# A three-block opening, a refetched half group and a shift added by TensorE in a hybrid encoder block

## The chip, the cores and the metric

The kernel runs on one core of a Trainium2 chip. The metric is the time of one execution on the device in microseconds (us). Engines are called by their names: TensorE (PE) multiplies matrices, with its weight loads shown apart as PEld; VectorE (DVE) and ScalarE (ACT) work element by element; GpSimd (POOL) does so too; SyncE (SP) issues transfers from memory. The profile also shows the clock that was granted to TensorE, as a share of the full one.

## What is computed

One layer of an encoder on 256 tokens of 2048 channels, in float32. The reference, cut to its skeleton:

```python
proj = h @ w_in[l]
q, k, v, r, af, ab, hy_u, gate_logits = jnp.split(proj, split_idx, axis=-1)
y_gla = _gla_branch(q, k, v, r, af, ab, ...)      # gated linear attention, both directions
y_hy = _hyena_branch(hy_u, ...)                   # two long convolutions by FFT, gated
g = jax.nn.sigmoid(gate_logits...)
merged = g[:, :, 0, :] * (y_gla @ w_gla_o[l]) + g[:, :, 1, :] * (y_hy @ w_hy_o[l])
mix = merged @ w_out[l]
h = _layernorm(DEEPNORM_ALPHA * h + mix, ln1_g[l], ln1_b[l])
ff = jnp.square(jax.nn.relu(h @ w_ff1[l])) @ w_ff2[l]
h = _layernorm(DEEPNORM_ALPHA * h + ff, ln2_g[l], ln2_b[l])
```

Nearly all of the arithmetic is in products with weight matrices. The two layer norms stand where all channels of a token must be known before anything can go on.

## The kernel before

The tokens form two tiles of 128. All weights lie in memory as blocks of 128 x 2048 numbers (1 MB each), in the order in which they are used. `fetch` (line 89) brings the next block into one of three `raw` buffers by a transfer on SP's queue and splits each half of it in two (`split_hi_lo`, line 80): ScalarE rounds the half to a shorter format (`whi`), and VectorE subtracts that from the original (`wlo`). There are three buffers for split halves. A product then takes a high and a low part, so that float32 accuracy comes from fast products: hi x hi, hi x lo and lo x hi.

There are two ways to use a block. `channel_pair` (line 133) makes channels by tokens: a pair of products for each of the 16 k tiles, one 512 wide (lines 143 and 373: both parts of the activations at once) and one 256 wide (lines 144 and 374). `token_group` with `token_products` (line 151) makes tokens by channels: 512 channels from four blocks, three 512-wide products for each k tile and token tile. `column_products` (line 778) does the same with 256 channels at a time. `fetch`ing runs one block ahead of the products, and side work (filters, attention, convolutions) is hung onto the stream of blocks by `later` and `pump`: each block counts as one tick. The order of the instructions on each engine is then set by a scheduler that simulates a timeline, so source order is not instruction order, but on each engine the order is fixed.

The stages that matter here, in order:

- Opening (lines 209 to 221 and 367 to 378). Three warm-up products; then block 0 and x in halves on SP, the block's first half, then two quarters of x, and so on. x becomes `xT`, split in two parts. The products of block 0 (`pa`) follow k tile by k tile; blocks 1 and 2 are the first two of q. `filt_consts` (line 237) loads nine small constants by ScalarE's queue.
- Filters and attention: `filt_layer`, `filt_time` and `filt_freq` make the long filters beside the q, k and r blocks; the attention runs beside the v blocks.
- Inverse transform (`hy_inv`, line 650): 16 times, 12 products of 256 columns, six for each token tile.
- w_out and the first norm (lines 803 to 834): groups 0 to 2 of four blocks each, for both token tiles; group 3 keeps three of its blocks resident in split form (`resident`, line 743), so that tile 0 can be finished ahead of tile 1, 256 channels at a time. `add_mix` adds the residual and takes statistics, `norm_scale` (line 760) makes scale and shift, `norm_chunk` (line 771) applies them: one ScalarE step, then a multiplication by the row ln1_g and an addition of ln1_b on VectorE, for one chunk of 512 channels on POOL. `turn` transposes a chunk on TensorE and splits it into `hT`.
- ff1 and ff2 in quarters. The first block of ff1 takes tile 0 first and tile 1 then (`by_tile`).
- End (lines 874 to 886): the last group of ff2, with four resident blocks, tile 0 and then tile 1; the second norm by the same `norm_chunk`, and six stores for each tile.

Of the kernel before, what the change touches and what calls it, by code (L numbers as in the profile page):

```python
# [16 lines left out]
P = 128  # L17
# [23 lines left out]
def block_kernel(  # L41
# [42 lines left out]
    nblk = wblk.shape[0]  # L84
# [4 lines left out]
    def fetch(between=lambda n, h: None):  # L89
        n = fetched[0]  # L90
        if n >= stop_at[0]:
            return
        fetched[0] = n + 1
        raw = wp.tile([P, D], F32, tag="raw", bufs=3, name=f"raw{n}")
        if n > 1:
            nc.sync.dma_start(raw, wblk[n])
        parts = []
        for h in range(2):
            if n <= 1:
                hs = slice(h * D // 2, (h + 1) * D // 2)  # L100
                nc.sync.dma_start(raw[:, hs], wblk[n][:, hs])
                between(n, h)
            hi = wp.tile([P, D // 2], F32R, tag="whi", bufs=3, name=f"whi{n}_{h}")
            lo = wp.tile([P, D // 2], F32R, tag="wlo", bufs=3, name=f"wlo{n}_{h}")
            split_hi_lo(hi, lo, raw[:, h * 1024:(h + 1) * 1024])
            parts.append((hi, lo))
        queue.append(parts)

# [24 lines left out]
    def channel_pair(act, name, dst=None, scale=1.0, by_tile=False):  # L133
        if dst is None:
            dst = base.tile([P, 2, L], F32, tag="sum", name=f"{name}_s")
        for c in range(2):
            ps = psum_main(f"{name}_{c}").rearrange("p (a b) -> p a b", a=2)
            parts = next_block()
            for ts in ((slice(0, P), slice(P, L)) if by_tile and c == 0 else (slice(0, L),)):
                for kt in range(KT):  # L140
                    hi, lo = parts[kt // 8]
                    js = slice(kt % 8 * P, (kt % 8 + 1) * P)
                    MM(ps[:, :, ts], hi[:, js], act[:, kt, :, ts], start=(kt == 0), stop=False)  # L143
                    MM(ps[:, 0, ts], lo[:, js], act[:, kt, 0, ts], start=False, stop=(kt == KT - 1))  # L144
            low = base.tile([P, L], F32, tag="low", name=f"{name}_l{c}")
            nc.scalar.activation(low, ps[:, 1], AF.Copy, scale=scale)
            nc.vector.scalar_tensor_tensor(dst[:, c], ps[:, 0], scale, low, op0=ALU.mult, op1=ALU.add)
            pump()
        return dst
# [58 lines left out]

    with tc.tile_pool(name="xp", bufs=1) as xp:
        def load_x(n, h):  # L210
            for g in (2 * h, 2 * h + 1):
                xr = xp.tile([P, 4, L], F32, tag=f"xr{g}", name=f"xr{g}")
                nc.sync.dma_start(xr, xt[:, 4 * g:4 * g + 4, :])
                split_hi_lo(xT[:, 4 * g:4 * g + 4, 0], xT[:, 4 * g:4 * g + 4, 1], xr)
# [6 lines left out]
        fetch(load_x)  # L221
# [15 lines left out]
    def filt_consts():  # L237
        raw = fp.tile([P, 4, P], F32, tag="w4", name="dftraw")
        nc.scalar.dma_start(raw, dft_in)
        split_hi_lo(dfth, dftl, raw)  # L240
        mw = fp.tile([P, 3, P], F32, tag="mlpw", name="mlpw")
        nc.scalar.dma_start(mw, mlp_w)
        mc = fp.tile([P, 4], F32, tag="mlpc", name="mlpc")
        nc.scalar.dma_start(mc, mlp_c)
        et = fp.tile([P, L], F32, tag="emb", name="emb_sb")
        nc.scalar.dma_start(et, emb)
        nc.scalar.dma_start(ba_sb, ba)
        nc.scalar.dma_start(conv_sb, convp)
        nc.scalar.dma_start(mask_sb, mask_in)
        nc.scalar.dma_start(sgn_sb, sgn_in)  # L250
        nc.scalar.dma_start(ident, ident_in)
        fst["mw"], fst["mc"], fst["g"] = mw, mc, et
# [113 lines left out]

    pa = psum_main("pa").rearrange("p (a b) -> p a b", a=2)
    fetch()
    parts = next_block()
    for kt in range(KT):  # L370
        hi, lo = parts[kt // 8]
        js = slice(kt % 8 * P, (kt % 8 + 1) * P)
        MM(pa, hi[:, js], xT[:, kt], start=(kt == 0), stop=False)
        MM(pa[:, 0], lo[:, js], xT[:, kt, 0], start=False, stop=(kt == KT - 1))
# [7 lines left out]
    k_sb = qp.tile([P, 8, L], F32, tag="k", name="k_sb")  # L382
    for dst, nm, sc in ((q_sb, "q", 1.0 / 16.0), (k_sb, "k", 1.0)):
        for c2 in range(4):
            channel_pair(xT, f"{nm}{c2}", dst[:, 2 * c2:2 * c2 + 2, :], sc)
# [357 lines left out]
    def resident(slots):  # L743
        parts = []
        for hi, lo in slots:
# [3 lines left out]
            nc.sync.dma_start(raw, wblk[n])  # L749
# [18 lines left out]

    CHUNKS = ((0, 256), (256, 256), (1536, 512), (512, 512), (1024, 256), (1280, 256))

    def norm_chunk(z, rows, tb, at, n, rs, nb):
        zc = z[:, tb, at:at + n]
        eng = nc.gpsimd if at == 1536 else nc.vector
        nc.scalar.activation(zc, zc, AF.Identity, scale=rs, bias=nb)
        eng.tensor_tensor(zc, zc, rows[:, 0, at:at + n], op=ALU.mult)
        eng.tensor_tensor(zc, zc, rows[:, 1, at:at + n], op=ALU.add)
# [26 lines left out]
    for g in range(3):  # L803
        pss = token_group(mT, f"wo{g}")
        for tb in range(NT):
            add_mix(pss[tb], tb, g * 512, 512)
    x0 = tuple(ep.tile([P, D], F32R, tag=t, name=t) for t in ("xh", "xl"))
    parts = resident([x0] + halves(ep, "f", "wr1"))
    pss = [[psum_main(f"wo3_{tb}{ch}") for ch in range(2)] for tb in range(NT)]
    column_products(pss, mT, [queue.popleft()], range(NT), 0)  # L810
    stop_at[0] = nblk
    hT = act_tile(ep, "hT", "hT")
    for tb in range(NT):
        column_products(pss, mT, parts, [tb], 1)
        if tb == 1:
            fetch()
# [12 lines left out]

        for at, n in CHUNKS:  # L830
            norm_chunk(z1, rows1, tb, at, n, rs, nb)
            if at < 1536:
                turn(at, n)
        turn(1536, 512)
# [4 lines left out]
    def ff1(qi):  # L839
        f = act_tile(ep, "f", f"f{qi}") if qi % 2 == 0 else act_tile(base, "xT", f"f{qi}")  # L840
        for c2 in range(8):
            r = channel_pair(hT, f"f{qi}_{c2}", by_tile=(qi == 0 and c2 == 0))
# [7 lines left out]
    def add_ff(ps, tb, at, n, qi):  # L850
# [26 lines left out]
    pss = [[psum_main(f"w2_33_{tb}{ch}") for ch in range(2)] for tb in range(NT)]  # L877
    for tb in range(NT):
        column_products(pss, fts[3], parts, [tb], 0)
        with tc.high_priority():  # L880
            for ch in range(2):
                add_ff(pss[tb][ch][:, 0:256], tb, 1536 + ch * 256, 256, 3)
            rs, nb = norm_scale(st2, tb, "2")
        for at, n in CHUNKS:
            norm_chunk(z1, rows2, tb, at, n, rs, nb)
            nc.sync.dma_start(out[tb * P:(tb + 1) * P, at:at + n], z1[:, tb, at:at + n])
# [127 lines left out]
```

## Time and profile before

| | us |
|---|---|
| median of 3 runs | 1893.24 (1892.57 to 1893.65) |
| the profiled execution | 1891.83 |
| its span, first to last instruction | 1890.0 |
| TensorE busy | 1860.4 |
| VectorE busy | 1313.6 |
| ScalarE busy | 949.5 |
| POOL busy | 38.3 |
| moved from and to memory | 375.09 MB, 198 GB/s on average |

The mean granted clock is 0.994. In rows of the timeline the columns are: start, duration, engine, line, operation, output <- input, shape, count, and in brackets the idle time of the engine just before and what ended it. In rows of windows: the stretch, its length, the busy time of PE, PEld, DVE, ACT and POOL with the number of instructions, the granted clock, the share of the DMA engines and GB/s. A row of a group has busy time and mean duration in ns. Products overlap in the records; what one costs is seen from start to start.

### The profile page before, as it was taken

How to read it: one execution, taken by the hardware profiler on the slowest of the kernel's cores; microseconds unless marked ns; L12 is line 12 of the kernel's file. 1: busy time of each engine (PE TensorE's matmuls, PEld its weight loads, DVE VectorE, ACT ScalarE, POOL GpSimd, SP SyncE). 2: the span in 40 equal slices, each digit the busy share in tenths (PEclk: the TensorE clock that was granted, in tenths of full speed). 3: DMA queues.
4: the chain of work that ended last, by engine and by line, in shares of the span. 5: the costliest groups of instructions: out<-in, count | busy, mean ns of one | idle time of the engine just before them, and what ended most of it. 6: DMA issues, size and time to landing. Idle time of an engine off the chain costs nothing.

```text
span 1890.0 us, 25333 instructions
## 1 busy us (share of the span) xinstructions
PE 1860.4 (98%) x10060; PEld 1599.7 (85%) x10060; DVE 1313.6 (70%) x1702; ACT 949.5 (50%) x1286; POOL 38.3 (2%) x60
## 2 busy tenths in 40 slices
PE   8999999999999999999999998999999999999996
PEld 7887888888888888888888888888888888888886
DVE  6787968875789888888556567666555555555556
ACT  5555556674555555555544444444434443444343
POOL 0000000000000000000000001000000000000001
PEclk9999999999999999999999999999999999999998
DMA  7667764445555555565655764555555555545552
GB/s 289 231 225 251 265 228 161 140 142 204 195 195 199 199 194 189 197 223 191 212 197 183 285 216 153 188 193 186 196 186 198 180 199 187 192 180 199 191 189 110
DMA packets 60583, 375.09 MB, mean 198 GB/s; under 512 B 7216, under 2 KB 10928, under 8 KB 20912
## 3 DMA queue, kind: packets, MB, share of 16 engines
q1 hardware_dynamic: 46512, 324.03, 47.4%
q0 software_dynamic: 5888, 29.36, 4.2%
q10 hardware_dynamic: 8064, 20.07, 3.0%
q8 instruction: 79, 1.29, 0.3%
q14 instruction: 40, 0.33, 0.0%
HBM read 356.66 MB, written 16.78 MB: 198 GB/s over the span
## 4 chain that ended last, share of the span: by engine, by line
PE 93%; DVE 4%; ACT 1%; DMA 1%; issue 1%; ACTq 0%; DVEq 0%; SPq 0%
PE f L143 13%; PE f L144 6%; PE g L143 6%; PE w L163 6%; PE w L164 6%; PE w L162 6%; PE go L143 3%; PE ux L143 3%; PE uz L143 3%; PE uv L143 3%; PE g L144 3%; PE ho L143 3%; PE ho L144 2%; PE uv L144 2%; PE ux L144 2%; PE go L144 2%
## 5 line engine op out<-in xcount | busy, mean ns | idle before, releaser
L82 DVE TENSOR_TENSOR wlo<-raw,whi 128x1024 fp32r<-128x1024 f32 x596 | 728.3, 1223 | 488.2 <-ACT whi L81 487.3
L81 ACT CAST whi<-raw 128x1024 fp32r<-128x1024 f32 x596 | 627.0, 1053 | 772.6 <-PE w L164 186.8
L143 PE MATMUL f<-hT,whi 128*128 128x512 f32 (+1 forms) x1040 | 361.7, 394 | 0.0
L144 PE MATMUL f<-hT,wlo 128*128 128x256 f32 (+1 forms) x1040 | 290.0, 279 | 0.0
L143 PEld LDWEIGHTS f<-hT,whi 128*128 128x128 f32 x1040 | 195.6, 188 | 44.3
L144 PEld LDWEIGHTS f<-hT,wlo 128*128 128x128 f32 x1040 | 197.1, 190 | 0.1
L163 PE MATMUL w<-wlo,f 128*128 128x512 f32 x480 | 186.8, 389 | 0.0
L164 PE MATMUL w<-whi,f 128*128 128x512 f32 x480 | 186.8, 389 | 0.0
L143 PE MATMUL g<-xT,whi 128*128 128x512 f32 x512 | 178.6, 393 | 0.0
L162 PE MATMUL w<-whi,f 128*128 128x512 f32 x480 | 168.0, 389 | 0.0
L144 PE MATMUL g<-xT,wlo 128*128 128x256 f32 x512 | 143.5, 281 | 0.0
L143 PEld LDWEIGHTS g<-xT,whi 128*128 128x128 f32 x512 | 95.7, 187 | 21.1
L162 PEld LDWEIGHTS w<-whi,f 128*128 128x128 f32 x480 | 90.0, 188 | 18.8
L164 PEld LDWEIGHTS w<-whi,f 128*128 128x128 f32 x480 | 90.1, 188 | 18.7
L163 PEld LDWEIGHTS w<-wlo,f 128*128 128x128 f32 x480 | 90.1, 188 | 18.5
L144 PEld LDWEIGHTS g<-xT,wlo 128*128 128x128 f32 x512 | 96.7, 189 | 0.5 <-DVE wlo L82 0.2
L143 PE MATMUL uz<-xT,whi 128*128 128x512 f32 x256 | 91.9, 398 | 0.0
L143 PE MATMUL ux<-xT,whi 128*128 128x512 f32 x256 | 91.7, 398 | 0.0
L143 PE MATMUL go<-yg,whi 128*128 128x512 f32 x256 | 91.1, 397 | 0.0
L143 PE MATMUL uv<-xT,whi 128*128 128x512 f32 x256 | 90.5, 395 | 0.0
L143 PE MATMUL ho<-yh,whi 128*128 128x512 f32 x256 | 88.8, 391 | 0.0
L144 PE MATMUL ux<-xT,wlo 128*128 128x256 f32 x256 | 72.0, 281 | 0.0
(329 smaller groups left out, 3336.7 us busy)
## 6 DMA issues: line engine op xcount, KB each, us to landing
raw<-wblk SPq DMA_DIRECT2D x303, 1024.0 KB, 4.8
Td<-T POOLq DMA_DIRECT2D x16, 768.0 KB, 4.1
Tl<-Td POOLq DMA_DIRECT2D x16, 768.0 KB, 4.5
w<-w4s ACTq DMA_DIRECT2D x16, 512.0 KB, 4.6
zr<-ln_rows ACTq DMA_DIRECT2D x4, 1024.0 KB, 10.9
raw<-wblk SPq DMA_DIRECT2D x4, 512.0 KB, 6.7
xr<-xt SPq DMA_DIRECT2D x4, 512.0 KB, 6.5
dec<-decay_in ACTq DMA_DIRECT2D x8, 256.0 KB, 3.1
```

The lines of the kernel that those rows point to most:

```text
L81: nc.scalar.copy(hi, src)
L82: nc.vector.tensor_tensor(lo, src, hi.bitcast(F32), op=ALU.subtract)
L143: MM(ps[:, :, ts], hi[:, js], act[:, kt, :, ts], start=(kt == 0), stop=False)
L144: MM(ps[:, 0, ts], lo[:, js], act[:, kt, 0, ts], start=False, stop=(kt == KT - 1))
L162: MM(pss[tb], sh, wh, start=(kt == 0), stop=False)
L163: MM(pss[tb], sh, wl, start=False, stop=False)
L164: MM(pss[tb], sl, wh, start=False, stop=(kt == KT - 1))
```

## The change

- Opening. x and the first three blocks (the gates' block and the first two of q) are loaded in quarters, interleaved, all on SP: group g holds 512 columns of each block and four k tiles of x, and for group 0 the pieces of block 0 and x are halved again. Each group's products for the three blocks are made as it arrives, into three PSUM tiles (`open_ps`) that stay open over the four groups. The fourth block is fetched after them. The constants move from ScalarE's queue to POOL's.
- Second part of w_out. Group 2's last two blocks are used for token tile 0 only; after group 3 they are fetched again (`AGAIN`) and used for tile 1. Group 3 is made in 512-wide products. The norm has chunks of 256, 256, 512, 512 and 512, and POOL takes no part in it.
- The first two blocks of ff1 (`channel_pair_by_tokens`) take tile 0 for three halves, then tile 1 for these, then the fourth half for both.
- `hy_inv`: six products of 512 columns in place of 12 of 256.
- Second norm. The multiplication by ln2_g is made right after the last addition to each chunk (`add_ff`). What is left is scale * z + (shift * ln2_g + ln2_b). Tile 0's last group is 512 wide, and two VectorE steps a chunk apply the norm (`affine`). For tile 1 the bracket is made on TensorE in plain float32: ident x ln2_b ahead of the statistics, then diag(shift) x ln2_g on top; one VectorE step a chunk remains.

```diff
-    def fetch(between=lambda n, h: None):
+    AGAIN = [W_OUT_END - 6, W_OUT_END - 5]
+    stream = list(range(W_OUT_END)) + AGAIN + list(range(W_OUT_END, wblk.shape[0]))
+    def fetch():
...
+    def channel_products(ps, act, half, kts, ts=FULL, opens=True):
+        hi, lo = half
+        for kt in kts:
+            js = slice(kt % 8 * P, (kt % 8 + 1) * P)
+            MM(ps[:, :, ts], hi[:, js], act[:, kt, :, ts], start=(kt == 0 and opens), stop=False)
+            MM(ps[:, 0, ts], lo[:, js], act[:, kt, 0, ts], start=False, stop=(kt == KT - 1))
...
+    def channel_pair_by_tokens(act, name):
...
+        for ts in (slice(0, P), slice(P, L)):
+            for c, h in ((0, 0), (0, 1), (1, 0)):
+                channel_products(ps[c], act, blocks[c][h], range(8 * h, 8 * h + 8), ts,
+                                 opens=(c == 0 or ts.start == 0))
+        channel_products(ps[1], act, blocks[1][1], range(8, KT))
...
+        for g in range(4):
+            n = 2 if g == 0 else 1
+            for i in range(n):
+                load_w(0, g, i, n)
+                load_x(g, i, n)
+            for b in range(1, OPENING):
+                load_w(b, g, 0, 1)
+        for g in range(4):
...
+                channel_products(open_ps[b], xT, halves_of[b], range(4 * g, 4 * g + 4))
...
-        nc.scalar.dma_start(raw, dft_in)
+        nc.gpsimd.dma_start(raw, dft_in)
...
-            for tb in range(NT):
-                dst = py[:, tb * CW:(tb + 1) * CW]
-                mm3(dst, dfth[:, 2], dftl[:, 2], yh[:, tb, 0], yl[:, tb, 0], True, False)
-                mm3(dst, dfth[:, 3], dftl[:, 3], yh[:, tb, 1], yl[:, tb, 1], False, True)
+            mm3(py3, dfth[:, 2], dftl[:, 2], yh[:, :, 0], yl[:, :, 0], True, False)
+            mm3(py3, dfth[:, 3], dftl[:, 3], yh[:, :, 1], yl[:, :, 1], False, True)
...
+    for b in range(4):
+        token_products(pss2, mT, [next_block()], range(NT) if b < 2 else [0], b)
+    add_mix(pss2[0], 0, 1024, 512)
...
+        token_products(pss3, mT, parts, [tb], 1)
         with tc.high_priority():
-            for ch in range(2):
-                add_mix(pss[tb][ch][:, 0:256], tb, 1536 + ch * 256, 256)
+            add_mix(pss3[tb], tb, 1536, 512)
+        if tb == 0:
+            for _ in range(2):
+                fetch()
+        else:
+            for b in range(2, 4):
+                token_products(pss2, mT, [next_block()], [1], b)
+        with tc.high_priority():
+            if tb == 1:
+                add_mix(pss2[1], 1, 1024, 512)
             rs, nb = norm_scale(st1, tb, "1")
...
+            nc.vector.tensor_tensor(zc, zc, rows2[:, 0, at:at + n], op=ALU.mult)
...
+    column_products([None, pss], fts[3], parts, [1], 0)
+    for at, n in CHUNKS:
+        po[at] = psum_side(f"lo{at}")[:, 0:n]
+        tc.keep_in_program_order(MM(po[at], ident, rows2[:, 1, at:at + n], start=True, stop=False))
...
+    nc.vector.tensor_scalar(dg, ident, nb, None, op0=ALU.mult)
+    affine(1, 0, 256, rs, nb)
+    store(1, 0, 256)
+    for at, n in CHUNKS:
+        MM(po[at], dg, rows2[:, 0, at:at + n], start=False, stop=True)
+        zc = z1[:, 1, at:at + n]
+        nc.vector.scalar_tensor_tensor(zc, zc, rs, po[at], op0=ALU.mult, op1=ALU.add)
+        store(1, at, n)
```

More of the change, by code (lines that the diff above doesn't have):

```diff
@@ L94, in fetch @@
         raw = wp.tile([P, D], F32, tag="raw", bufs=3, name=f"raw{n}")
-        if n > 1:
-            nc.sync.dma_start(raw, wblk[n])
+        nc.sync.dma_start(raw, wblk[stream[n]])
         parts = []
         for h in range(2):
[L99 to L104, printed above, removed]
+            hi, lo = weight_half(n, h)
             split_hi_lo(hi, lo, raw[:, h * 1024:(h + 1) * 1024])
@@ L107, in fetch, with weight_half @@
         queue.append(parts)
+    def weight_half(n, h):
+        return (wp.tile([P, D // 2], F32R, tag="whi", bufs=3, name=f"whi{n}_{h}"),
+                wp.tile([P, D // 2], F32R, tag="wlo", bufs=3, name=f"wlo{n}_{h}"))
     side = []
@@ L136, in channel_pair @@
         for c in range(2):
-            ps = psum_main(f"{name}_{c}").rearrange("p (a b) -> p a b", a=2)
+            ps = channel_psum(f"{name}_{c}")
             parts = next_block()
[L139 to L147, printed above, removed]
+            for h in range(2):
+                channel_products(ps, act, parts[h], range(8 * h, 8 * h + 8))
+            channel_sum(dst[:, c], ps, f"{name}_l{c}", scale)
+            pump()
+        return dst
+    def channel_pair_by_tokens(act, name):
+        dst = base.tile([P, 2, L], F32, tag="sum", name=f"{name}_s")
+        ps = [channel_psum(f"{name}_{c}") for c in range(2)]
+        blocks = [next_block() for _ in range(2)]
+        for ts in (slice(0, P), slice(P, L)):
[3 more added lines that the diff above has]
+        channel_products(ps[1], act, blocks[1][1], range(8, KT))
+        for c in range(2):
+            channel_sum(dst[:, c], ps[c], f"{name}_l{c}")
             pump()
@@ L206, in block_kernel @@
     qp = qkg.enter_context(tc.tile_pool(name="qp", bufs=1))
+    OPENING = 3
+    open_ps = [channel_psum(f"open{b}") for b in range(OPENING)]
     with tc.tile_pool(name="xp", bufs=1) as xp:
[L210 to L214, printed above, removed]
         wu = xp.tile([P, 512], F32, tag="wu", name="wu")
@@ L220, in block_kernel, with load_x, load_w @@
             MM(pw, wu[:, 0:P], wu, start=True, stop=True)
-        fetch(load_x)
+        raws = [wp.tile([P, D], F32, tag="raw", bufs=3, name=f"raw{b}") for b in range(OPENING)]
+        fetched[0] = OPENING
+        xr = [xp.tile([P, 4, L], F32, tag=f"xr{g}", name=f"xr{g}") for g in range(4)]
+        halves_of = [None] * OPENING
+        def load_x(g, i, n):
+            step = 4 // n
+            nc.sync.dma_start(xr[g][:, step * i:step * (i + 1)], xt[:, 4 * g + step * i:4 * g + step * (i + 1), :])
+        def load_w(b, g, i, n):
+            cs = slice(512 * g + 512 // n * i, 512 * g + 512 // n * (i + 1))
+            nc.sync.dma_start(raws[b][:, cs], wblk[b][:, cs])
+        for g in range(4):
[6 more added lines that the diff above has]
+        for g in range(4):
+            pieces = 2 if g == 0 else 1
+            for b in range(OPENING):
+                if g % 2 == 0:
+                    halves_of[b] = weight_half(b, g // 2)
+                hi, lo = halves_of[b]
+                n = pieces if b == 0 else 1
+                w, step = 512 // n, 4 // n
+                for i in range(n):
+                    at = 512 * (g % 2) + w * i
+                    cs = slice(512 * g + w * i, 512 * g + w * (i + 1))
+                    split_hi_lo(hi[:, at:at + w], lo[:, at:at + w], raws[b][:, cs])
+                    if b == 0:
+                        ks = slice(4 * g + step * i, 4 * g + step * (i + 1))
+                        split_hi_lo(xT[:, ks, 0], xT[:, ks, 1], xr[g][:, step * i:step * (i + 1)])
+                channel_products(open_ps[b], xT, halves_of[b], range(4 * g, 4 * g + 4))
     nc.vector.memset(ones_sb, 1.0)
@@ L364, in block_kernel @@
         later(n + 2, filt_freq(c, o))
[L367 to L374, printed above, removed]
+    pa = open_ps[0]
     nc.scalar.copy(a_low, pa[:, 1])
@@ L748, in resident @@
             raw = wp.tile([P, D], F32, tag="raw", bufs=3, name=f"raw{n}")
-            nc.sync.dma_start(raw, wblk[n])
+            nc.sync.dma_start(raw, wblk[stream[n]])
             for h in range(2):
@@ L767, in norm_scale @@
         return rs, nb
[L769 to L776, printed above, removed]
     def column_products(pss, act, blocks, tbs, b0):
@@ L801, in add_mix @@
             nc.vector.bn_stats(st1[:, tb, at // 256 + i, :], zc[:, i * 256:(i + 1) * 256])
-    for g in range(3):
+    for g in range(2):
         pss = token_group(mT, f"wo{g}")
@@ L828, in turn @@
             split_hi_lo(dst[0], dst[1], pt[:, 0:n].rearrange("p (a b) -> p a b", b=P))
[L830 to L834, printed above, removed]
+        for at, n in ((0, 256), (256, 256), (512, 512), (1024, 512), (1536, 512)):
+            zc = z1[:, tb, at:at + n]
+            nc.scalar.activation(zc, zc, AF.Identity, scale=rs, bias=nb)
+            nc.vector.tensor_tensor(zc, zc, rows1[:, 0, at:at + n], op=ALU.mult)
+            nc.vector.tensor_tensor(zc, zc, rows1[:, 1, at:at + n], op=ALU.add)
+            turn(at, n)
     fts = {}
```

75 lines of the change are left out of this document (48 added, 27 removed).

## The prediction

> **What bounds the kernel now.** I read the page's busy shares and the chain that ended last, then the timeline at the places where TensorE is not fed.
>
> ```profile
> PE 1860.4 (98%) x10060; PEld 1599.7 (85%) x10060; DVE 1313.6 (70%) x1702; ACT 949.5 (50%) x1286; POOL 38.3 (2%) x60
> PE 93%; DVE 4%; ACT 1%; DMA 1%; issue 1%; ACTq 0%; DVEq 0%; SPq 0%
> ```
>
> TensorE is the bound: 29.6 us of the 1890.0 us span are not its own. A change can only win in those gaps, in stretches at the half clock, or by needing less TensorE time. The largest places are the opening, the first norm and the end, which are the three that are edited. First the opening (timeline; the last two rows are windows, in which the number after POOL's is the granted clock):
>
> ```profile
> 5.74 1.04 ACT L81 CAST whi<-raw 128x1024 fp32r<-128x1024 f32 x1 [2.31 <-DMA raw<-wblk]
> 9.36 1.05 ACT L81 CAST xT<-xr 128x1024 fp32r<-128x1024 f32 x1 [0.40 <-DMA xr<-xt]
> 10.27 0.79 PE L373 MATMUL pa<-xT,whi 128*128 128x512 f32 x1 [3.89 <-DVE xT L82]
> 10.86 0.41 PE L374 MATMUL pa<-xT,wlo 128*128 128x256 f32 x1
> 11.50 0.41 PE L374 MATMUL pa<-xT,wlo 128*128 128x256 f32 x1
> 14.90 1.05 ACT L81 CAST whi<-raw 128x1024 fp32r<-128x1024 f32 x1 [0.39 <-DMA raw<-wblk]
> 18.53 0.40 PE L143 MATMUL q<-xT,whi 128*128 128x512 f32 x1
> 22.07 0.40 PE L143 MATMUL q<-xT,whi 128*128 128x512 f32 x1
> 28.75 0.70 PE L259 MATMUL mlp<-emb_sb,mlpw 33*128 33x256 f32 x2
> 30.65 0.39 PE L143 MATMUL q<-xT,whi 128*128 128x512 f32 x1
> 9.00:9.50 0.50, 0.00 (x0) 0.00 (x0) 0.50 (x1) 0.14 (x1) 0.00 (x0) 0.56 1.02 387
> 15.50:16.00 0.50, 0.50 (x4) 0.44 (x3) 0.28 (x2) 0.45 (x1) 0.00 (x0) 0.62 1.07 451
> ```
>
> The first product waits until 10.27 for x to be split. The clock halves at about 9.05 and is full again at about 15.9; in between a pair of products (one k tile) takes 11.50 - 10.86 = 0.64 us, afterwards (22.07 - 18.53)/10 = 0.354. Three weight blocks are done at 30.65, of which 0.70 is a filter product that the change puts elsewhere: 29.95. Transfers of 512 KB land 1.39 us apart (four intervals from 9.36 to 14.90), 0.38 MB/us.
>
> Now the first norm (line 817 to the first two blocks of ff1), with its windows:
>
> ```profile
> 1145.25 0.42 DVE L799 SCALAR_TENSOR_TENSOR zr<-zr,wo 128x256 f32<-128x256 f32 x1 [2.70 <-PE wo L792]
> 1147.77 0.16 DVE L766 SCALAR_TENSOR_TENSOR lnb<-mv,lrs 128x1 f32<-128x1 f32 x1
> 1157.60 0.36 PE L143 MATMUL f<-hT,whi 128*128 128x256 f32 x1
> 1160.64 0.34 PE L143 MATMUL f<-hT,whi 128*128 128x256 f32 x1
> 1162.37 1.47 POOL L775 TENSOR_TENSOR zr<-zr 128x512 f32<-128x512 f32 x1 [9.78 <-DVE zr L776]
> 1163.03 2.76 DVE L775 TENSOR_TENSOR zr<-zr 128x512 f32<-128x512 f32 x2 [0.32 <-ACT zr L774]
> 1167.70 0.56 PE L143 MATMUL f<-hT,whi 128*128 128x256 f32 x1
> 1168.17 0.52 PE L143 MATMUL f<-hT,whi 128*128 128x256 f32 x1
> 1179.64 0.37 ACT L146 ACTIVATE f_l<-f 128x256 f32<-128x256 f32 x1
> 1161.00:1162.50 1.50, 0.04 (x1) 0.01 (x1) 1.31 (x4) 1.50 (x4) 0.14 (x1) 1.00 0.00 0
> 1162.50:1163.00 0.50, 0.48 (x3) 0.36 (x4) 0.21 (x1) 0.50 (x2) 0.50 (x1) 0.76 0.00 0
> 1169.00:1170.00 1.00, 1.00 (x7) 0.86 (x6) 0.31 (x1) 0.00 (x0) 0.00 (x0) 0.71 1.07 451
> ```
>
> The reader is to see that token tile 1's norm is not covered: TensorE ends tile 0's products at 1161.0, starts tile 1's at 1167.70 and is at the half clock until about 1169.6. VectorE's two 512-wide multiplications take 2.76 us while POOL works on the same tile. The two blocks of ff1 are done at 1179.5, which is 34.3 us after the last product of tile 0's last group (1145.25). A pair of half width costs (1160.64 - 1157.60)/13 = 0.234.
>
> **The change, part by part.** Prices of single steps:
>
> ```profile
> 523.08 0.28 PE L227 MATMUL yp<-Yl,dfth 128*128 128x256 f32 x1
> 523.56 0.28 PE L228 MATMUL yp<-Yh,dftl 128*128 128x256 f32 x1
> 1129.07 0.39 PE L164 MATMUL wo<-whi,mT 128*128 128x512 f32 x1
> 1129.75 0.39 PE L164 MATMUL wo<-whi,mT 128*128 128x512 f32 x1
> 1130.37 0.68 DVE L799 SCALAR_TENSOR_TENSOR zr<-zr,wo 128x512 f32<-128x512 f32 x1
> 1130.96 1.22 DVE L82 TENSOR_TENSOR wr<-raw,wr 128x1024 fp32r<-128x1024 f32 x1
> 1132.10 0.68 DVE L799 SCALAR_TENSOR_TENSOR zr<-zr,wo 128x512 f32<-128x512 f32 x1
> 1132.70 0.74 DVE L801 BATCH_NORM_STATS2 bst<-zr 128x6 f32<-128x256 f32 x2
> raw<-wblk SPq DMA_DIRECT2D x303, 1024.0 KB, 4.8
> 350.00:360.00 10.00, 9.07 (x40) 7.18 (x40) 10.00 (x25) 6.07 (x10) 0.00 (x0) 1.00 0.27 93
> ```
>
> From start to start a 256-wide product costs 0.12, a 512-wide one 0.227; on VectorE a step costs 0.60 at 512 wide and 1.14 at 1024.
>
> *Opening.* x and three blocks, 5.24 MB, come in 18 pieces on SP. The first product needs 0.39 MB; half a MB had landed by 5.74, then one cast and one subtraction follow: 6.9 (5.7 to 8.2). At 0.38 MB/us the four groups are complete at about 8.6, 12.1, 15.6 and 19.1. VectorE's work per group is 3 x 0.60 + 1.14 = 2.9 us (steps below), under the 3.5 of the transfers. TensorE needs 48 x 0.354 = 17.0. I add 0.9 for early waits (the second 0.39 MB come 1 us behind the first) and 1.5 for one stretch of 3.4 us, half of the one seen, at the half clock (5.3 pairs in place of 9.6): 26.3. That is 3.65 before the 29.95. What is late next is the fourth block: its transfer waits for block 0's buffer, free when its last quarter, which lands near 16.3, has passed ScalarE and VectorE (an estimate: 18.4); it lands 4.8 later and needs 1.05 and 1.22 for its first half's split: 25.5, or up to 1.5 later behind the constants that now wait on POOL's queue for x's buffers. I take 0.3 of idle. Opening: -3.4 (bounds -5.5 and 0).
>
> The constants' nine issues leave ScalarE's queue for POOL's, where nothing else stands until the filters are written; cost nothing, as the first filter product moves from the third block to the fifth. With it the whole filter work slides two blocks later and ends in the v groups, where TensorE already loses time to VectorE (9.07 busy of 10 in the last row, and VectorE full). Bounds +2 and -2, none taken, since the work is the same.
>
> *Inverse transform.* 16 x 12 products of 256 become 16 x 6 of 512: 96 x (0.24 - 0.227) = -1.2; beside 256-wide neighbours the step may be 0.24, which makes 0. I take -1.0.
>
> *First norm.* Group 3 in 512-wide products saves 96 x 0.013 = 1.2. Behind tile 0's last product stand 23 of tile 1's and 24 refetched ones, 47 x 0.227 = 10.7 instead of 72 x 0.12 = 8.6, so that point (call it T) comes 1.2 + 2.1 = 3.3 us earlier. Against it VectorE now gets after T, in the order of its instructions: tile 0's add, statistics, scale (3.3 us, the 2.68 from 1145.25 to 1147.93 and 0.6 for the wider chunk), the first activation (0.6), ten norm steps (4.9), the adds and statistics of two tile 1 groups (2.5), four 1024-wide splits (4.6; before, the blocks were split ahead of T) and tile 0's transposed splits (2.5): with the waits between them about 18.9. Then tile 1's scale, activation, ten norm steps and five splits, now without POOL beside them: 28.8. TensorE can start tile 1 at T + 26.1. Tile 0's cover ends at T + 21.5, so the clock falls again; 24 half-width pairs (5.5) and eight full ones (2.8) with 2.5 of half clock end at T + 36.9, that is 33.6 after the old T against 34.3. First norm: -0.7 (bounds -3.1, if the clock stays up, and +2, if VectorE's chain has gaps of that size). The two extra transfers hide: SP has nothing else there.
>
> *End.*
>
> ```profile
> 1875.64 0.42 DVE L855 TENSOR_TENSOR zr<-zr,w 128x256 f32<-128x256 f32 x1 [1.69 <-PE w L792]
> 1878.16 0.16 DVE L766 SCALAR_TENSOR_TENSOR lnb<-mv,lrs 128x1 f32<-128x1 f32 x1
> 1884.50 0.74 DVE L776 TENSOR_TENSOR zr<-zr 128x256 f32<-128x256 f32 x2
> out<-zr SPq DMA_DIRECT2D x8, 128.0 KB, 2.3
> ```
>
> Tile 0's last group in 512-wide products: 48 x 0.013 = -0.6. Behind the last product VectorE ends at 1885.24, 9.6 us later, with the last store after it (unchanged). Now: the 2.68 to the shift, plus one 512-wide step of tile 0 and one 256-wide multiplication ahead of it (0.9), the diagonal (0.25), two 256-wide steps (0.85), while the four shift products run. The trace has the 256-wide plain-float32 product at 0.70, so I put 512 at 0.9 (1.7 at half clock). They end at 4.8, 5.65, 6.5 and 7.0, each followed by one VectorE step of 0.6: the last ends at 7.7. The four products with rows of ln2_b run from 0 to 3.1 and keep the clock up. End: -1.9 (bounds -2.2 and +1).
>
> Sum: -3.4 - 1.0 - 0.7 - 0.6 - 1.9 = -7.6. The profiled execution took 1891.83 (its span 1890.0 and 1.83 around it), 1.4 under the median 1893.24 of the runs; I put 1884.2 for it and 1885.6 for the median.
>
> **Where a rule speaks otherwise.** In the trace the clock fell near 1162.75 though TensorE had been idle for 1.5 us only (1161.00:1162.50) after a busy stretch. The Trainium skill (TensorE: Matmul & The Clock Gate, "Why this matters for your kernels") asks only for no idle gap above some 3 us; by it the transposes between T + 21.5 and T + 26.1 would hold the clock up and the sum would be about 2.5 us lower; the row disagrees.
>
> In the trace 512 KB transfers land 1.39 us apart, as fast as whole blocks need. The Trainium skill (DMA: Bandwidth & Descriptors, "Anatomy of one DMA" and "Bandwidth") gives each transfer about 2 us fixed and asks for 1 MiB at least. Were that cost paid in turn, 18 pieces would take 36 us more, an estimate from that page that the rows speak against.
>
> **Rivals.**
> 1. *VectorE's chain wins at the first norm, or in the v groups* (+2 there in place of -0.7, +1 in the v groups): 1889.3. For it: VectorE is full there in the windows. Against it: POOL's interference is gone.
> 2. *The clock stays up* through the opening and the first norm (-1.5, -2.5 less what phase gives back, say -3): 1882.6. For it: the warm-up products now run into the first real ones. Against it: the fall at 1162.75.
> 3. *Small pieces land slowly* (the other side). If each of the 18 pieces lands d after the one before, from 5.0 on, the fourth block starts at 5.0 + 17d + 2.75 + 2.3 (the last piece, one MB at 0.38 MB/us, the split). At d = 1.39, the rate of pieces twice the size, that is 33.7: the opening loses 3.7, and 1.5 of clock, and the whole change comes to +1.0, 1894.2, no change. From d of 1.6 it is slower; at 1.7 it starts at 38.95 and the total is 1899.5. Against it: the last number of the two clock windows of the opening, 387 and 451 GB/s, with several transfers in flight.
> 4. *The opening gains nothing*, since the fourth block is late by what the start won: 1889.0.
>
> **How the numbers follow.** Forecast 0.50 (its own range 1883 to 1888.5); rival 1 0.17; rival 2 0.14; rival 4 0.08; rival 3 0.11, of which 0.07 slower. A measurement here tells about 0.2%, 3.8 us, from no change, so faster ends at 1889.45. Rivals 1 and 4 lie on that edge; I count half of each as faster: 0.50 + 0.14 + 0.12 = 0.76. Slower 0.07, same 0.17. The range leaves out rival 3 and a little at each end: 1881 to 1891.
>
> **What would show it.** Right: first product near 7, three blocks done near 26, no idle above 1 us ahead of the fourth; a start-to-end time from T to the second block of ff1 near 37 with T 3 us earlier; VectorE's last step 7.7 after the last product; inverse-transform products 0.227 apart. Wrong: pieces more than 1.2 us apart, a gap ahead of the fourth block, a second half-clock stretch in the opening, plain-float32 products at 1.7 at the end, or more lost in the v groups.

## The result: 1898.26 us, slower by 0.26%

The changed kernel takes 1898.26 us (median of 16 runs, 1890.81 to 1901.41); the kernel before took 1892.47 beside it (16 runs). The ratio is 1.0026, with a 95% interval from 1.0019 to 1.0033. The prediction was 1885.6 with a range of 1881 to 1891. The profiled execution has a span of 1896.7, 6.7 above the span before; the page of the changed kernel begins with

```profile
span 1896.7 us, 24933 instructions
PE 1872.2 (99%) x9852; PEld 1592.0 (84%) x9852; DVE 1319.7 (70%) x1713; ACT 946.8 (50%) x1282; POOL 30.8 (2%) x61
```

TensorE has 208 recorded products fewer than before and is busy 11.8 us longer. Of these, 6.4 are the new plain-float32 products of the end (3.17 and 3.27, shown further below). Apart from these the recorded products have exactly as many columns in all as before, since the merged ones are wider; so the rest is that products take longer, and the stages tell where. The starts of stages (timeline; uv: first product of the long convolutions, ho: after them, then w_out, the third block of ff1, the first block of ff2, and the last product), first before, then changed:

```profile
472.64 0.39 PE L143 MATMUL uv<-xT,whi 128*128 128x512 f32 x1
976.59 0.39 PE L143 MATMUL ho<-yh,whi 128*128 128x512 f32 x1
1065.34 0.39 PE L162 MATMUL wo<-whi,mT 128*128 128x512 f32 x1
1178.60 0.39 PE L143 MATMUL f<-hT,whi 128*128 128x512 f32 x1
1345.00 0.39 PE L162 MATMUL w<-whi,f 128*128 128x512 f32 x1
1875.32 0.28 PE L792 MATMUL w<-wr,f 128*128 128x256 f32 x1
```

```profile
27.35 0.40 PE L142 MATMUL q<-xT,whi 128*128 128x512 f32 x1
476.02 0.39 PE L142 MATMUL uv<-xT,whi 128*128 128x512 f32 x1
980.33 0.40 PE L142 MATMUL ho<-yh,whi 128*128 128x512 f32 x1
1070.77 0.40 PE L187 MATMUL wo<-whi,mT 128*128 128x512 f32 x1
1185.55 0.40 PE L142 MATMUL f<-hT,whi 128*128 128x512 f32 x1
1355.15 0.40 PE L187 MATMUL w<-whi,f 128*128 128x512 f32 x1
1884.84 0.28 PE L835 MATMUL w<-wr,f 128*128 128x256 f32 x1
```

The first row of the second list is the fourth block, which began at 30.65 before, behind a filter product of 0.70. The differences, with that product counted where it now stands:

| stage | predicted | measured |
|---|---|---|
| opening, three blocks | -3.4 | -2.6 |
| fourth block to uv (filters, attention) | 0 | +6.0 |
| long convolutions, uv to ho | -1.0 | +0.4 |
| ho to w_out | 0 | +1.7 |
| w_out and first norm, two blocks of ff1 | -0.7 | +1.5 |
| rest of ff1's first two quarters | 0 | +3.2 |
| ff2 and the rest, to the last product | -0.6 | -0.6 |
| behind the last product | -1.9 | -2.8 |
| sum | -7.6 | +6.8 (span: +6.7) |

Two losses stand out, of different kinds. The first is a wait. In the changed kernel (timeline, with the POOL queue's issue that starts it, and windows: length, busy PE, PEld, DVE, ACT, POOL, then the granted clock):

```profile
22.34 0.54 POOL L295 DMA_DIRECT2D dftraw<-dft_in  x1 [18.32 <-DVE xT L82]
23.92 0.54 POOL L302 DMA_DIRECT2D emb_sb<-emb  x1
382.69 0.39 PE L284 MATMUL o<-vh,stl 128*128 128x512 f32 x1
385.53 1.28 DVE L82 TENSOR_TENSOR vl<-v,vh 128x512 fp32r<-128x512 f32 x2
386.27 0.50 PE L142 MATMUL g<-xT,whi 128*128 128x512 f32 x1 [3.20 <-DVE vl L82]
383.00:386.00 3.00, 0.07 (x1) 0.00 (x0) 3.00 (x8) 2.98 (x11) 0.00 (x0) 1.00 0.02 5
386.00:392.00 6.00, 5.73 (x23) 4.90 (x24) 6.00 (x20) 4.06 (x11) 0.00 (x0) 0.72 0.00 0
```

TensorE stands idle for 3.2 us, with VectorE and ScalarE full, and pays for it again at the half clock: a mean clock of 0.72 over 6 us is another 1.7. It waits for `vl`, the split of the last v group, which frees the PSUM tile that the third block of g writes to (four such tiles, line 70). The split comes in two steps, one for each token tile, and the first, which ended at 386.21, frees the tile. It is late since `vh` and `vl` have one buffer each, which the attention of the head before still reads (its last product starts at 382.69 and ends at 383.07); behind that, ScalarE and VectorE get to the split only after other attention work that stands ahead of it in their order. Before, these were in time:

```profile
378.48 0.39 PE L228 MATMUL o<-vh,stl 128*128 128x512 f32 x1
382.51 1.27 DVE L82 TENSOR_TENSOR vl<-v,vh 128x512 fp32r<-128x512 f32 x2
384.38 0.39 PE L143 MATMUL g<-xT,whi 128*128 128x512 f32 x1
15.85 0.34 ACTq L239 DMA_DIRECT2D dftraw<-dft_in  x1
17.18 0.46 ACTq L246 DMA_DIRECT2D emb_sb<-emb  x1
```

The first step of the split ended at 383.19, and the block began at 384.38: 1.2 us to spare. What covered the split then was a whole block: in TensorE's order the second block of g stood between the attention's last product (378.48) and the third block. In the changed kernel the attention comes one block later, and nothing stands between them. The chain goes back to the constants of the filter network: they reuse the memory of x's buffers, so they are issued when x's last quarter has been split: 23.92 where it was 17.18, and the first filter product comes at 36.15 where it was 28.75.

The second loss is no wait. In stretches where TensorE is never idle and at full clock, a pair of products (512 and 256 wide) comes every 0.347 us before and every 0.353 in the changed kernel. Windows of TensorE alone (busy, number of products that touch the window, clock), before and then changed:

```profile
985.00:1060.00 75.00, 75.00 (x434) 1.00 0.51 187
1190.00:1340.00 150.00, 150.00 (x867) 1.00 0.53 190
1445.00:1520.00 75.00, 75.00 (x426) 1.00 0.54 192
```

```profile
985.00:1060.00 75.00, 75.00 (x426) 1.00 0.49 183
1190.00:1340.00 150.00, 150.00 (x851) 1.00 0.50 185
1445.00:1520.00 75.00, 75.00 (x427) 1.00 0.51 189
```

Fewer products in the same busy time: 16 in 150 us. The same in single rows of the stage ho, three pairs in 1.03 us before and in 1.05 changed. The 256 pairs of the stage take 1065.34 - 976.59 = 88.75 us before and 1070.77 - 980.33 = 90.44 changed, 0.3467 and 0.3533 for one; I call the two the quick and the slow rhythm.

```profile
1010.22 0.39 PE L143 MATMUL ho<-yh,whi 128*128 128x512 f32 x1
1011.25 0.39 PE L143 MATMUL ho<-yh,whi 128*128 128x512 f32 x1
```

```profile
1010.36 0.40 PE L142 MATMUL ho<-yh,whi 128*128 128x512 f32 x1
1011.41 0.40 PE L142 MATMUL ho<-yh,whi 128*128 128x512 f32 x1
```

ff1's third and fourth quarters (the 1445 row) have the slow rhythm in both kernels. The two stages that differ, with the pairs of g ahead of ho, make 1.7 + 3.2 + 1.2 us.

### The profile page after: what moved, and what is told of

It is laid out like the page before. It is cut to its first block, busy times and chain, and to the rows that moved or that the text cites. A ratio compares the mean times of both kernels' runs of the same rounds, so it can differ in the third digit from the quotient of the medians.

```text
span 1896.7 us, 24933 instructions
## 1 busy us (share of the span) xinstructions
PE 1872.2 (99%) x9852; PEld 1592.0 (84%) x9852; DVE 1319.7 (70%) x1713; ACT 946.8 (50%) x1282; POOL 30.8 (2%) x61
## 4 chain that ended last, share of the span: by engine, by line
PE 87%; issue 8%; DVE 3%; ACT 1%; DMA 1%; POOL 0%; SPq 0%; DVEq 0%; POOLq 0%; ACTq 0%
PE f L142 13%; PE f L143 6%; PE g L142 6%; PE w L187 6%; PE w L188 6%; PE w L189 6%; PE ho L142 3%; PE ux L142 3%; PE go L142 3%; PE uz L142 3%; PE uv L142 3%; PE g L143 3%; PE uz L143 2%; PE uv L143 2%; PE ho L143 2%
## 5 line engine op out<-in xcount | busy, mean ns | idle before, releaser
L82 DVE TENSOR_TENSOR wlo<-raw,whi 128x1024 fp32r<-128x1024 f32 (+2 forms) x607 | 733.5, 1210 | 484.0 <-ACT whi L81 482.1
L81 ACT CAST whi<-raw 128x1024 fp32r<-128x1024 f32 (+2 forms) x607 | 631.8, 1042 | 773.5 <-PE w L189 186.2
L142 PE MATMUL f<-hT,whi 128*128 128x512 f32 (+1 forms) x1048 | 366.9, 398 | 0.0
```

Of the source, the lines that this page charges most:

```text
L81: nc.scalar.copy(hi, src)
L82: nc.vector.tensor_tensor(lo, src, hi.bitcast(F32), op=ALU.subtract)
```

## The experiments

The theory: (1) late filters push the attention against the v groups, which costs the 6.0; (2) the rhythm of a stretch of pairs costs some 6 more in the profile, and what is edited ahead of the stretch decides it. The rivals: the 6.0 come from bringing the blocks forward, whatever the filters do, or from other parts; the rhythm falls by chance in each execution.

**Both kernels profiled once more**, unedited.

> The kernel before, profiled a second time. In the first profile a pair of products (512 and 256 wide) came every 0.3467 us in the stretches 910-1065 and 1180-1345, and every 0.3533 us in 1430-1520 and 1610-1700. If the rhythm of a stretch is fixed by the program (by what stands ahead of it), the same four values return. If it falls by chance in each execution, at least one of the four changes. Nothing else should move.

> The changed kernel, profiled a second time. The first profile had 0.3533 us for a pair in all four stretches (905-1070, 1186-1355, 1442-1532, 1620-1710); against the first profile of before this is 1.1 + 1.7 + 3.2 us. Rhythm fixed by the program: 0.3533 in all four again, and a span near 1896.7. Rhythm by chance: some stretch at 0.3467, and a span shorter by 0.0067 us for each of its pairs (up to 12 us shorter). The wait of 3.2 us at 383, and the fall of the clock behind it, are in the order of VectorE and come again in both theories.

Spans 1891.1 and 1897.6. In all four stretches each kernel has the rhythm that it had, and the wait near 384 comes again (3.58 us from the start of the attention's last product to that of the block, both times). The first norm's stage took 114.6 in the kernel before, 1.3 more than in the first profile; so differences of that size in this stage say nothing. The rhythm by chance in each execution has two profiles of each kernel against it so far.

**The opening alone**, in the kernel before (all other hunks undone).

```diff
-    AGAIN = [W_OUT_END - 6, W_OUT_END - 5]
+    AGAIN = []
```

> The kernel before with the opening of the changed one alone (quarters of three blocks, constants on POOL's queue); w_out, the norms, ff1 and the inverse transform as before. Theory late filters: the constants wait for x's buffers until 22 us, the first filter product comes at 36 instead of 29, the whole filter and attention work runs 8 us late against the blocks, and VectorE cannot give it back: three blocks done at 27.3, but the first product of the long convolutions (uv) starts near 476 instead of 472.6, with a wait near 383. The time is then 2 to 4 us above before, apart from the rhythm of the pairs. Rival, the loss at 383 comes with the other parts of the change: uv starts near 469.5 and the time is 2 to 3 us below before.

1897.77, ratio 1.0020 (1.0011 to 1.0029), 5.0 above before where 2 to 4 were expected. The fourth block starts at 26.82, uv at 475.04:

```profile
384.25 0.79 PE L142 MATMUL g<-xT,whi 128*128 128x512 f32 x1 [3.19 <-DVE vl L82]
475.04 0.39 PE L142 MATMUL uv<-xT,whi 128*128 128x512 f32 x1
```

The wait belongs to the opening: from the fourth block to uv the kernel loses 5.5 us by it, of the 6.0 of the changed kernel. All pairs from 910 on kept the rhythm of before in this profile: the opening does not set it.

**The constants early**, in the changed kernel.

```diff
+    cstk = ExitStack()
+    cp = cstk.enter_context(tc.tile_pool(name="cp", bufs=1))
...
-        mw = fp.tile([P, 3, P], F32, tag="mlpw", name="mlpw")
+        mw = cp.tile([P, 3, P], F32, tag="mlpw", name="mlpw")
```

(and so `mlpc` and `emb`).

> The changed kernel with the three small constants of the filter network in a pool of their own, so that they do not wait for x's buffers; nothing else is edited. The first filter products then stand in the opening, and the attention work takes the places among the blocks that it has in the kernel before. Theory late filters: no wait above 1.5 us near 383, no fall of the clock there, uv starts near 470 (476.0 in the changed kernel), and the time is about 6 us below the changed kernel (near 1892). Rival, VectorE has too little time whatever the order, since the opening brings the blocks forward: uv stays near 474 to 476, and the time within 2 us of the changed kernel.

1890.90, ratio to before 0.9987 (0.9978 to 0.9997), 7.4 below the changed kernel's median:

```profile
9.27 0.70 PE L318 MATMUL mlp<-emb_sb,mlpw 33*128 33x256 f32 x2
383.00:386.00 3.00, 3.00 (x19) 2.63 (x18) 2.97 (x5) 3.00 (x8) 0.00 (x0) 1.00 0.00 0
473.15 0.40 PE L142 MATMUL uv<-xT,whi 128*128 128x512 f32 x1
```

The first filter product stands at 9.27 (36.15 in the changed kernel), and the window that was empty is full. uv came later than expected in this profile: its opening had a wait of 2.76 us for x and a stretch at the half clock, and the fourth block began at 29.74. From there to uv it took 443.4 us, where the changed kernel took 448.7. In the next runs with this opening uv starts at 469.7 to 471.3.

**The filters late**, in the kernel before: the cause alone, without the opening.

```diff
-        later(1 + l, filt_layer(l))
-    later(3, filt_hidden)
+        later(5 + l, filt_layer(l))
+    later(7, filt_hidden)
...
-        n = 4 + (i * 21) // 15
+        n = 8 + (i * 21) // 15
```

> The kernel before with all filter work due four blocks later than written, which puts the filter products and those of the first two heads into the same places of TensorE's order that they have in the changed kernel (first filter product behind 147 others in place of 91, first long-filter product behind 332 in place of 268). The opening is that of before. Theory late filters: the delay alone makes the loss, so uv starts 3 to 6 us later than 472.6, with a longer wait between 290 and 420, and the time is 3 to 6 us above before. Rival, the loss comes from bringing the blocks forward, whatever the filters do: uv within 1 us of 472.6, and no change in the time.

1897.57, ratio 1.0021 (1.0010 to 1.0031):

```profile
387.56 0.79 PE L143 MATMUL g<-xT,whi 128*128 128x512 f32 x1 [3.19 <-DVE vl L82]
476.34 0.39 PE L143 MATMUL uv<-xT,whi 128*128 128x512 f32 x1
```

The same wait appears with the old opening, and most of the loss: from the fourth block to uv 446.98 us, 4.3 more than before when the filter product, which now stands behind the fourth block, is counted, against 6.0 in the changed kernel. In the medians the loss is 5.3. With this the first part of the theory is shown from both sides; the rival that the loss comes from bringing the blocks forward has fallen, though a part of up to 1.7 us may still be due to it.

**All but the opening.** The changed kernel with the opening hunks undone.

> The changed kernel with the opening of before and the constants on ScalarE's queue again; all other parts as changed. Theory: the loss of 6 us between 30 and 470 belongs to the opening alone, so uv starts at 472.6 as before, without the wait of 3.2 near 383; the end keeps its gain of 3.5, w_out and the first norm come to 114.7 as changed; what the long convolutions and ff1 lose depends on the rhythm (0.3533 in 905 to 1070 and in ff1: 6 us). Time 1894.5 with the slow rhythm in both, 1889 with the fast one in both. Rival, the parts work on each other (VectorE at the first norm): the stage from w_out to the third block of ff1 differs from 114.7 by more than 1.5.

1892.65, ratio 0.9999 (0.9990 to 1.0008); uv at 471.41, no wait near 383, the first norm's stage 114.64, the end gains 3.5, and the slow rhythm in ho and ff1. The time is 1.9 below the 1894.5 expected with that rhythm. The other parts together change nothing that can be measured.

**The inverse transform as before** (twelve products of 256), on top of the early constants.

> The kernel with the early constants, with the inverse transform back at twelve products of 256 columns. Theory rhythm (a pair of products takes 0.3467 or 0.3533 us, and what stands ahead of a stretch of pairs decides which): with the last products of the long convolutions as in the kernel before, the stretches 905 to 1070 fall back to 0.3467, 445 pairs gain 3.0 and the inverse transform loses 0.6: 2.4 us less than with the early constants (near 1888.5). Rival, the slower rhythm of that stretch comes from something else (the opening's place, the clock): 0.3533 stays and the time rises by 0.6.

1889.19, ratio to before 0.9985 (0.9977 to 0.9994). In the profile the stretch came back to the quick rhythm, and ff1, which was not edited, kept the slow one:

```profile
985.00:1060.00 75.00, 75.00 (x435) 1.00 0.52 193
1190.00:1340.00 150.00, 150.00 (x851) 1.00 0.50 186
```

Against the run with the early constants the medians fell by 1.7 where 2.4 were expected; the ratios to before, 0.9987 and 0.9985, hardly differ. So the switch is seen in one profile, its price in the runs is not shown.

**w_out, first norm and ff1's first block as before**, on top of the early constants.

> The kernel with the early constants, with w_out, the first norm and the first block of ff1 as before (no refetched blocks, POOL takes part again). My prediction gave that part -0.7; the profiles show 113.3 and 114.6 for the stage before and 114.8, 114.6 and 115.0 changed. Theory: the refetch gains nothing, the stage comes to 113.3 to 114.7, and ff1's first half goes back to 0.3467 a pair (-3.2): 3 to 4 us less than with the early constants (near 1887.5). Rival, the refetch is worth its 0.7 and the rhythm of ff1 comes from elsewhere: the time rises by 0.7.

1888.47, ratio 0.9978 (0.9969 to 0.9988), 2.4 below the early constants where 3 to 4 were expected, with intervals that overlap. The stage took 114.06, and this time ff1 switched and ho did not:

```profile
985.00:1060.00 75.00, 75.00 (x426) 1.00 0.50 183
1190.00:1340.00 150.00, 150.00 (x867) 1.00 0.51 190
```

Over the profiles with ordinary pairs (none turned round as in the last experiments) the stage from w_out to the third block of ff1 took 114.0 to 115.0 with the refetch (five) and 113.3 to 114.7 without (seven): no gain.

**A break ahead of ff1's third and fourth quarter**, in the kernel before.

```diff
+        if qi in BEATS:              # {2: 4, 3: 2}
+            beat = psum_side(f"beat{qi}")
+            for _ in range(BEATS[qi]):
+                tc.keep_in_program_order(MM(beat[:, 0:P], ident, ident, start=True, stop=True))
```

> The kernel before with nothing but four idle products of 128 columns (ident by ident into a PSUM tile that nobody reads) put ahead of the third quarter of ff1, and two ahead of the fourth. In all profiles so far both quarters ran at 0.3533 a pair, after groups of 512-wide products. Theory rhythm: a break decides it, so at least one of the quarters goes to 0.3467, 255 pairs gain 1.7 us each block of sixteen pairs times 0.107, that is 1.7 us for a quarter, and the time falls by 1.5 for each quarter that changes, less 0.7 for the products. Rival, it belongs to these quarters (their buffers, their weights): both stay at 0.3533 and the time rises by 0.7.

1893.47, ratio 1.0006 (0.9997 to 1.0015). The theory fell here: both quarters stayed at the slow rhythm. And ff1's first half, ahead of the edit, with TensorE's products in the same order as before, had the slow rhythm in this profile:

```profile
1190.00:1340.00 150.00, 150.00 (x851) 1.00 0.49 184
1445.00:1520.00 75.00, 75.00 (x427) 1.00 0.52 186
```

So not every break decides it, and one order can have either rhythm. This profile is of the longest of the run's twelve executions (1899.27). The stretch of g ahead of uv (422 to 470) says the same in other profiles: in four kernels with the early constants TensorE has the same order of products up to 520 us, and two ran this stretch at the slow rhythm (274 products; the early constants alone, and the first of the last two runs below), two at the quick one (279; with the inverse transform as before, and with w_out as before). So the order of TensorE's products alone does not fix it.

**Every second pair turned round**, in the kernel before: 512, 256, 256, 512 wide.

```diff
-                    MM(ps[:, :, ts], hi[:, js], act[:, kt, :, ts], start=(kt == 0), stop=False)
-                    MM(ps[:, 0, ts], lo[:, js], act[:, kt, 0, ts], start=False, stop=(kt == KT - 1))
+                    wide = lambda: MM(ps[:, :, ts], hi[:, js], act[:, kt, :, ts], start=(kt == 0), stop=(kt == KT - 1))
+                    narrow = lambda: MM(ps[:, 0, ts], lo[:, js], act[:, kt, 0, ts], start=False, stop=False)
+                    for product in ((wide, narrow) if kt % 2 == 0 else (narrow, wide)):
+                        product()
```

> The kernel before with every second pair of products turned round (512, 256, 256, 512 wide), the same products in all. It asks what the slower rhythm hangs on. If it is the alternation of one wide and one narrow product with a weight load behind each, the turned order knows neither 0.3467 nor 0.3533 but one value of its own, the same in all stretches. If two rhythms remain, two narrow products in a row are no cure: two values again, and a time that differs from before by less than 6 us either way. If a narrow product is too short to hide the load of the next weights when another narrow one follows, all pairs cost more: 0.02 a pair or more, 40 us in all.

1889.14, ratio 0.9979 (0.9968 to 0.9990). One value in all stretches, 0.3483 (89.17 us for the 256 pairs of ho):

```profile
985.00:1060.00 75.00, 75.00 (x432) 1.00 0.51 189
1190.00:1340.00 150.00, 150.00 (x863) 1.00 0.50 189
1445.00:1520.00 75.00, 75.00 (x433) 1.00 0.50 192
```

**What gains, together.** First the opening, the early constants and the end; then these with the merged inverse transform and turned pairs.

> What the runs so far show to gain, put together: the opening by quarters with the early constants and the new end; the inverse transform, w_out, the first norm and the first block of ff1 as in the kernel before. Theory: the stage up to uv comes to 470 (before 472.6), 905 to 1070 and the first half of ff1 run at 0.3467 a pair, the end is 3.5 shorter: about 6 us below before, near 1886.3. Rival, the parts share a gain (one rhythm changes with the other edit): 0.3533 in one of the stretches, and 1888 or more.

1886.36, ratio 0.9962 (0.9948 to 0.9976): fourth block 27.76, uv 471.01, quick rhythm in ho and ff1's first half, 11.45 behind the last product (14.65 before).

> The opening by quarters with early constants, the new end and the merged inverse transform, with every second pair of products turned round, and w_out, the first norm and ff1's first block as before. With turned pairs there was one value, 0.3483, in all stretches. Then the merged inverse transform cannot change the rhythm of what follows and keeps its 0.6, and the stretches that stood at 0.3533 fall to 0.3483: from the 1886.4 of the opening, early constants and end, the long convolutions gain 1.9 and 0.6, the last two quarters of ff1 1.3 each, and 905 to 1070 and ff1's first half lose 1.2 together: near 1882.5. Rival, the parts do not add: 1885 or more.

1881.47, ratio 0.9946 (0.9931 to 0.9960), the best of the runs and 16.8 below the changed kernel.

## Why the prediction was wrong

The step that failed is the second paragraph of the opening's part: "cost nothing, as the first filter product moves from the third block to the fifth", and the slide to the v groups with "bounds +2 and -2, none taken, since the work is the same". It measured +6.0. I had in front of me that the constants wait for x's buffers, and that VectorE is full there (10.00 busy of 10 us, TensorE 9.07), and priced the slide by the amount of work instead of asking who waits for its end: the buffers that the third head's attention reads, the split of the last v group that needs them and, through it, a PSUM tile. The margin was 1.2 us. Rival 1 named the place, but gave it +1.

The forecast of -7.6 and the measured +6.8 of the profile are 14.4 apart. Of these, 6.0 are this step, about 6.1 (1.2 + 1.7 + 3.2) the rhythm of the pairs, for which the sum had no term, 2.2 the first norm and 0.8 the opening; the end gave 0.9 back.

- Opening: the first product came at 5.80 (predicted 6.9), the fourth block had no wait ahead of it, the clock stayed full, and three blocks were done at 27.35 where I had 26.3. TensorE still waited 1.39, 0.32 and 1.52 us for x's and the first pieces. The kernels with the old opening began the fourth block at 29.3 to 30.7, so up to 1.4 of the gain over 30.65 is only the spread of the old opening. Rival 3 (small pieces land slowly) did not happen.
- Inverse transform: the products themselves gained 0.6 of the 1.0; the pairs behind them then ran at the slow rhythm, which no term of the sum had. With turned pairs, where there is one rhythm, the stage from uv to ho took 502.05 without the merged transform and 500.92 with it: 1.1 less in these two profiles, close to the 1.0 predicted.
- First norm: T is the addition at 1147.62, that is 76.9 behind the start of w_out (79.9 before), 3.0 earlier as predicted (3.3). The clock fell as predicted:

```profile
1147.62 0.69 DVE L842 SCALAR_TENSOR_TENSOR zr<-zr,wo 128x512 f32<-128x512 f32 x1 [0.26 <-PE wo L189]
1173.00:1176.00 3.00, 2.64 (x14) 2.43 (x13) 2.98 (x6) 1.17 (x2) 0.00 (x0) 0.50 0.74 300
```

  The two blocks were done 37.9 behind T (predicted 36.9). My mark for before was late: I took ScalarE's read at 1179.5 for the end of the two blocks, but the third began at 1178.60, 33.35 and not 34.3 behind T. 3.1 earlier and 4.6 longer make +1.5 in place of -0.7; over all profiles of this stage the refetch is worth nothing that stands out of their spread.
- End: right, and a little better. The last group gained 0.6; VectorE's last step ended 8.0 after the last product (predicted 7.7; 9.6 before), and what I had left unchanged behind it fell from 4.7 to 3.5. The plain-float32 products ran at the full clock (1.00 from 1884.9 to 1893), and a set of four, three 512 wide and one 256, took 3.17 and 3.27:

```profile
1884.96 3.17 PE L955 MATMUL lo<-zr,ident 128*128 128x512 f32 x8
1889.10 3.27 PE L964 MATMUL lo<-zr,dg 128*128 128x512 f32 x8 [0.96 <-DVE dg L960]
1890.26 2.86 DVE L966 SCALAR_TENSOR_TENSOR zr<-zr,lrs,lo 128x512 f32<-128x512 f32 x4 [0.30 <-PE lo L964]
```

- The rhythm: no step of the prediction had it. I took 0.354 for a pair throughout, from the opening, where the traces have 0.347 elsewhere; a look at these would have shown that a pair has more than one price.

What stays open: what sets the rhythm. In all five profiles with the merged inverse transform and ordinary pairs ho was slow, and in all seven without it quick; ff1's first half was slow in five of five with the first two blocks by tokens, and in one of seven without. So the edits go with the rhythm without fixing it. The mechanism was not found. How much the rhythm weighs in the median of the changed kernel was not measured apart from the profiles.

## What to carry to other kernels

When an edit moves side work, follow the last reader of each of its buffers to the engine that waits for it: the same work, begun 7.4 us later, cost 6, through a one-buffer tile and a PSUM tile with 1.2 us to spare. Constants that everything hangs on should not share memory with buffers that an edit may hold longer. If TensorE's busy time rises by more than the products that were added, count the products in a window without idle time: the price of one product may have changed.

## What was not expected of the hardware

A stream of 512- and 256-wide products, each with its own weights, ran at one of two steady rates, 0.3467 and 0.3533 us a pair, at the full clock and without idle time, and kept its rate for 65 to 170 us. With every second pair turned round it ran at 0.3483 in all these stretches, in both profiles. The Trainium skill (TensorE: Matmul & The Clock Gate, "Wait — 56ns, not 53.3ns?") gives each product at the full clock one fixed extra of about 2.5 ns over its columns; by it a pair would take 0.325 us, an estimate from that page. The traces, with a weight load for each product, have more, and two values, so the extra is not one number here.
